# Input projection of a hybrid encoder layer: seven block products in place of eight

## Chip, cores and metric

The kernel runs on one core of a Trainium2 chip. The metric is the device time of one execution in microseconds, a median over runs. TensorE is the matmul engine, VectorE (DVE) and ScalarE (ACT) work element by element, GpSimd (POOL) does little here, and SyncE (SP) issues all DMA transfers, in the order of its queue.

## What is computed

One encoder layer over two groups of 1024 tokens (a prompt and a sample) of width 1024. One matmul projects each token to 8736 columns, which four kinds of heads share; each runs a recurrence in both directions, and a second matmul, a layer norm and a gated input follow.

```
proj = jnp.einsum('btd,de->bte', x, w_in)          # 1024 x 1024 by 1024 x 8736, per group
pr, ph, pm, ps = jnp.split(proj, SPLITS, axis=-1)
mixed = jnp.concatenate([
    _retention(pr, ...),   # 4 heads: q, k (rotated), v, g
    _hgrn2(ph, ...),       # 4 heads: q, zf, zb, i, g
    _mlstm(pm, ...),       # 4 heads: q, k, v, o, g, and 16 gate columns
    _ssd(ps, ...),         # z, x, B, C (a convolution over tokens), and 16 gate columns
], axis=-1)
y = jnp.einsum('bte,ed->btd', mixed, w_out)
x = _layer_norm(DN_ALPHA * x + y, ln_g, ln_b)
gate = sigmoid(x @ w_ple_gate);  return x + gate * (p @ w_ple_proj)
```

## The kernel before

**Precision.** Each fp32 operand of a large matmul is held as two float32r parts, high and low, and a product is three matmuls: high by high, high by low, low by high. `split` (L162) makes the parts: a ScalarE copy for the high one, then a VectorE subtraction for the low one.

**Stages.** For each group the 14 units of `ORDER` (L37) run one after the other: four `hg`, then `ret`, `ssd` and `ml` mixed. A unit projects its own columns, runs its recurrence with fp32 matmuls of 128 columns (two TensorE instructions each, one for a transpose), normalises, transposes and stores 128 channels of the mix to DRAM (`norm_out`, L530; in the rows `hY` is the normalised block, `hZ` the stored one). After both groups come the output projection, layer norm and gate for four half groups.

**Projection.** `stream` (L318) loads a weight piece 512 columns at a time (`ws`) and splits it into `wh` and `wl`; the weights are loaded and split again for the second group. `proj_chan` (L356) gives channels on partitions: the weights are stationary, 512 tokens move, 24 matmuls into one bank `pj`, then an evacuation. `proj_tok` (L341) gives tokens on partitions: the tokens are stationary, 256 weight columns move (288 in `("ret", 0, "vg")`, which carries the gate columns). Retention's pairs, `v` and gates, mLSTM's `v` and `o` and SSD's `z` use the second form. Each bank is one chain of 24 matmuls and is evacuated once.

**Inputs.** `load_x` (L311) loads the 16 blocks of 128 channels by 512 tokens of a group and splits each (`xr` to `xh`, `xl`); the first projection takes them as they come in. `load_mix` does the same for the output stage.

**Order.** A scheduler places all instructions on the engines by priority, which follows the order of the code; `late` (L167) moves a piece, and weight splits go 600 places ahead (`EARLY`). Buffers come from pools: 10 of `p` (1032 columns), 7 of `r`, 12 of `h` (512 columns), 3 pairs of 1024 weight columns, 4 of `ws`, 4 + 4 PSUM banks (L33).

Of the kernel before, what the change touches and what calls it, by code (L numbers as in the profile page):

```python
# [9 lines left out]
F32 = mybir.dt.float32  # L10
# [18 lines left out]
KSC = 128.0 ** -0.5  # L29
ALPHA = 2.0 ** 0.25  # L30
LEVELS = (64, 32, 16, 8)
BLK = 8
PB, RB, HB, WB, SB, SSB = 10, 7, 12, 3, 4, 3  # L33
SLACK = [0, 0]
EARLY = 600
# [4 lines left out]
# column blocks of the input projection  # L40
# [7 lines left out]
def pieces():  # L48
    """(key, columns) of every piece of the input projection, in the order they are used."""
    out = []  # L50
    for g in range(2):
        out.append((("ssd", g, "z"), _blk(O_SSD + 256 * g, 256)))
        out.append((("ssd", g, "x"), _blk(O_SSD + 512 + 256 * g, 256)))
        out.append((("ssd", g, "bc"), _blk(O_SSD + 1024 + 128 * g) + _blk(O_SSD + 1280 + 128 * g)))
    for h in range(4):
        o = O_RET + 128 * h
        out.append((("ret", h, "qk"), _blk(o) + _blk(o + 512)))
        vg = _blk(o + 1024) + _blk(o + 1536)
        if h == 0:
            vg = vg + _blk(O_ML + 2560, 16) + _blk(O_SSD + 1536, 16)  # L60
        out.append((("ret", h, "vg"), vg))
        o = O_HG + 128 * h
        out.append((("hg", h, "qf"), _blk(o) + _blk(o + 512)))
        out.append((("hg", h, "b"), _blk(o + 1024)))
        out.append((("hg", h, "vg"), _blk(o + 1536) + _blk(o + 2048)))
        o = O_ML + 128 * h
        out.append((("ml", h, "qk"), _blk(o) + _blk(o + 512)))
        out.append((("ml", h, "g"), _blk(o + 2048)))
        out.append((("ml", h, "vo"), _blk(o + 1024) + _blk(o + 1536)))
    return out  # L70


IN_PIECES = pieces()
# [3 lines left out]
PIECE_AT = {}  # L77
_off = 0
for _d, _ps in ((D, IN_PIECES), (DI, OUT_PIECES), (D, GATE_PIECES), (PLE, PROJ_PIECES)):
# [8 lines left out]
# columns of the packed shape constants  # L88
K_ID, K_NF, K_NB, K_TF, K_TB, K_RF, K_RB, K_DF, K_DB, K_MF, K_MB = (
    0, 128, 256, 384, 385, 386, 387, 388, 516, 644, 772)  # L90
NKEEP, NCST = 388, 900


def constants():
# [13 lines left out]
    c[:, K_TB] = np.arange(P)  # L108
    m = np.zeros((P, 8, P), np.float32)
# [9 lines left out]
    rope = np.concatenate([cos, sin], 1).reshape(NCH, P, P).transpose(1, 0, 2)  # L119
# [4 lines left out]
def trunk(ctx, tc, xT, x, pT, wp, par_d, cst_d, msk_d, rope_d, out,  # L124
          groups=(0, 1), units=None, tail=True, dbg=None):
# [53 lines left out]
    with ExitStack() as c1:  # L179
        cp = c1.enter_context(tc.tile_pool(name="cp", bufs=1))  # L180
        xp = c1.enter_context(tc.tile_pool(name="xp", bufs=1))
        wq = c1.enter_context(tc.tile_pool(name="wq", bufs=WB))
        st = c1.enter_context(tc.tile_pool(name="st", bufs=SB))
# [30 lines left out]
        cst = par = msk = rope = ident = negm = nhalf = ones = rst = rate = None  # L214
        rrow = rkw = rdec = rD = fbt = ssa = cw = cb = lbw = low = oml = fsc = fbi = ksc = ksum = None

        def setup():
            """Constants, and what depends on the parameters alone."""
            nonlocal cst, par, msk, rope, ident, negm, nhalf, ones, rst, rate, rrow, rkw, rdec, rD
            nonlocal fbt, ssa, cw, cb, lbw, low, oml, fsc, fbi, ksc, ksum  # L220
# [1 line left out]
            cst = cp.tile([P, NKEEP], F32, name="cst")  # L222
            nc.sync.dma_start(cst, cst_d[:, 0:NKEEP])
# [9 lines left out]
            rope = cp.tile([P, NCH, P], F32, name="rope")  # L233
# [1026 lines left out]
```

## Time and profile before

| | us |
|---|---|
| median of 3 runs | 2708.0 (2707.66 to 2711.78) |
| span of the profiled execution | 2708.0 |
| TensorE busy (matmuls) | 2665.3 |
| VectorE busy | 1806.3 |
| ScalarE busy | 1095.3 |
| mean granted TensorE clock | 0.995 |

Busy time is the time in which an engine had an instruction under way; TensorE's matmuls overlap, so what one costs in a row of them is read from the distance between two starts. The granted clock is a share of full speed. The last normalised block of group 0 is written at 1086 us and that of group 1 at 2144 us.

### The profile page before, as it was taken

The numbers are of one execution on the slowest core, as the hardware profiler recorded it, in microseconds if no ns is written. First come the engines' busy times: TensorE is split into PE (matmuls) and PEld (weight loads), VectorE is DVE, ScalarE is ACT, GpSimd is POOL, SyncE is SP. The second block draws the span as 40 slices with busy tenths as digits, with TensorE's granted clock in tenths as the row PEclk, the third lists the DMA queues.
The fourth block names the chain that finished last, engine by engine and source line by source line (L and its number), as shares of the span: only waits on it lengthen the run. The fifth ranks groups of instructions, "written<-read, shape, count | busy, mean of one in ns | idle before, by whom it ended". The sixth has DMA issues, their size and how long they took to land.

```text
span 2708.0 us, 43819 instructions
## 1 busy us (share of the span) xinstructions
PE 2665.3 (98%) x16874; PEld 2384.2 (88%) x16874; DVE 1806.3 (67%) x4417; ACT 1095.3 (40%) x2197; POOL 55.6 (2%) x48
## 2 busy tenths in 40 slices
PE   9999999999999999999999999999999999999999
PEld 8889988879899999999898888989999888888887
DVE  7778768878755555787786878855455555546455
ACT  6656523444422313655533444432222343333323
POOL 0000000000000000000000000000000000000000
PEclk9999999999999999999999999999999999999999
DMA  4111011334321213111111241432122434535333
GB/s 148 47 41 39 24 51 41 94 94 94 86 71 48 78 40 105 44 48 35 41 38 41 75 105 51 91 105 67 56 63 89 164 121 136 190 122 195 128 113 105
DMA packets 172945, 225.15 MB, mean 83 GB/s; under 512 B 13888, under 2 KB 82112, under 8 KB 172736
## 3 DMA queue, kind: packets, MB, share of 16 engines
q1 hardware_dynamic: 172736, 222.34, 27.0%
q8 instruction: 133, 2.18, 0.3%
q14 instruction: 76, 0.62, 0.1%
HBM read 196.86 MB, written 25.43 MB: 82 GB/s over the span
## 4 chain that ended last, share of the span: by engine, by line
PE 93%; DVE 3%; DMA 2%; ACT 1%; issue 1%; POOL 0%; SPq 0%; DVEq 0%; ACTq 0%; POOLq 0%
PE pj L174 53%; PE po L174 13%; PE pg L174 7%; PE pov L177 5%; PE psc L177 5%; PE pst L177 4%; PE ptr L399 3%; PE pin L177 2%; PE pq L174 2%; DMA ub<-ud 1%; DMA ub<-fd 1%; DVE x L160 0%; DMA ws<-in_wp 0%; PE ptl L1125 0%; ACT wh L148 0%
## 5 line engine op out<-in xcount | busy, mean ns | idle before, releaser
L174 PE MATMUL pj<-wl,xh 128*128 128x256 f32 (+1 forms) x2304 | 664.2, 288 | 0.0
L174 PE MATMUL pj<-wh,xh 128*128 128x256 f32 (+1 forms) x2304 | 663.6, 288 | 0.3
L174 PE MATMUL pj<-wh,xl 128*128 128x256 f32 (+1 forms) x2304 | 662.7, 288 | 0.0
L151 DVE TENSOR_TENSOR wl<-ws,wh 128x512 fp32r<-128x512 f32 (+1 forms) x488 | 313.8, 679 | 303.0 <-ACT wh L148 299.8
L148 ACT ACTIVATE wh<-ws 128x512 fp32r<-128x512 f32 (+1 forms) x488 | 280.7, 617 | 468.3 <-PE pj L174 234.4
L174 PEld LDWEIGHTS pj<-wh,xh 128*128 128x128 f32 x2304 | 441.4, 192 | 2.6 <-DVE hB L154 1.1
L174 PEld LDWEIGHTS pj<-wl,xh 128*128 128x128 f32 x2304 | 441.6, 192 | 1.4
L174 PEld LDWEIGHTS pj<-wh,xl 128*128 128x128 f32 x2304 | 441.6, 192 | 0.6
L174 PE MATMUL pj<-xh,wh 128*128 128x512 f32 x1024 | 415.9, 406 | 5.8 <-ACT wh L148 5.8
L174 PE MATMUL pj<-xh,wl 128*128 128x512 f32 x1024 | 414.7, 405 | 0.0
L174 PE MATMUL pj<-xl,wh 128*128 128x512 f32 x1024 | 413.3, 404 | 0.0
L174 PEld LDWEIGHTS pj<-xh,wh 128*128 128x128 f32 x1024 | 194.2, 190 | 40.6 <-ACT wh L148 5.8
L174 PEld LDWEIGHTS pj<-xl,wh 128*128 128x128 f32 x1024 | 194.3, 190 | 34.7
L174 PEld LDWEIGHTS pj<-xh,wl 128*128 128x128 f32 x1024 | 194.1, 190 | 34.7 <-DVE wl L151 0.2
L174 PE MATMUL po<-wl,xh 128*128 128x512 f32 x512 | 202.9, 396 | 0.0
L174 PE MATMUL po<-wh,xh 128*128 128x512 f32 x512 | 202.1, 395 | 0.0
L174 PE MATMUL po<-wh,xl 128*128 128x512 f32 x512 | 202.1, 395 | 0.0
L174 PE MATMUL pg<-xn,wh 128*128 128x512 f32 x384 | 120.2, 394 | 0.0
L174 PEld LDWEIGHTS po<-wl,xh 128*128 128x128 f32 x512 | 96.2, 188 | 21.0
L174 PEld LDWEIGHTS po<-wh,xl 128*128 128x128 f32 x512 | 96.2, 188 | 20.4
L174 PEld LDWEIGHTS po<-wh,xh 128*128 128x128 f32 x512 | 96.2, 188 | 20.0 <-DVE g L157 0.2
L151 DVE TENSOR_TENSOR xl<-xr,xh 128x512 fp32r<-128x512 f32 x96 | 63.9, 690 | 68.5 <-ACT xh L148 66.5
(285 smaller groups left out, 4262.6 us busy)
## 6 DMA issues: line engine op xcount, KB each, us to landing
ws<-in_wp SPq DMA_DIRECT2D x472, 256.0 KB, 3.3
mix<-hZ SPq DMA_DIRECT2D x64, 256.0 KB, 2.8
ub<-fd SPq DMA_DIRECT2D x64, 256.0 KB, 7.3
ub<-ud SPq DMA_DIRECT2D x64, 256.0 KB, 7.1
xr<-mix SPq DMA_DIRECT2D x64, 256.0 KB, 5.1
xr<-in_xT SPq DMA_DIRECT2D x32, 256.0 KB, 5.1
xr<-in_x SPq DMA_DIRECT2D x32, 256.0 KB, 5.0
out<-sg SPq DMA_DIRECT2D x32, 256.0 KB, 2.0
```

Source lines behind the costliest of these rows:

```text
L148: S.activation(o, i, AF.Copy, scale=scale)
L151: V.tensor_tensor(o, a, b, op)
L174: TE.matmul(o, l, r, start=start, stop=stop)
L177: TE.matmul(o, l, r, start=start, stop=stop)
L399: TE.transpose(o[0:s.shape[1], P * n:P * n + s.shape[0]], s, ident[0:s.shape[0], 0:s.shape[0]])
```

## The change

**Seven products.** The input of a group is cut in four blocks (512 channels by 512 tokens: 11 and 12 for the first half of the tokens, 21 and 22 for the second), and the weights of two column blocks of 128 (a "quad") in four as well. Strassen's method, in Winograd's form, needs seven products of such blocks in place of eight: 11, 12, 22 and four sums S1 to S4 of input blocks, each with a weight block or a sum of them. There are 34 quads per group. A product is 12 matmuls of 512 columns with the weights stationary, so all results have channels on partitions.

```diff
+        def quad(g, key, ev_a, ev_b):
+            ws = quad_weights(key, g != groups[0])
+            def product(acc, b, start):
+                w = next(ws)
+                for j in range(4):
+                    h, l = X[b, j]
+                    wh, wl = w[:, P * j:P * j + P], w[:, 512 + P * j:512 + P * j + P]
+                    TE.matmul(acc, wh, h, start=start and j == 0, stop=False, skip_group_check=True)
+                    TE.matmul(acc, wh, l, start=False, stop=False, skip_group_check=True)
+                    TE.matmul(acc, wl, h, start=False, stop=j == 3, skip_group_check=True)
...
+            def held(acc):
+                t = sq.tile([P, 512], F32, tag="sq", name=nm("sq"))
+                with late(-EVAC):
+                    copy(t, acc)
+                return t
...
+            a, b = bank(), bank()
+            product(a, "11", True)
+            u1 = held(a)
+            product(b, "12", True)
+            ev_a(0, put(b, u1, ALU.add))
+            product(a, "S2", False)
+            u2 = held(a)
+            c = bank()
+            product(c, "S1", True)
+            product(a, "S3", False)
+            u3 = held(a)
+            ev_b(1, put(c, u3, ALU.subtract))
+            product(a, "22", False)
+            ev_a(1, put(a))
+            product(c, "S4", False)
+            ev_b(0, put(c, u2, ALU.subtract))
```

Bank `a` goes on adding after each of three copies to SBUF (`sq`, ScalarE); `put` combines two banks' sums in a VectorE addition or subtraction.

**Inputs.** `prep_x` takes the place of `load_x`. It loads 16 blocks, forms S1 to S4, splits seven kinds of blocks by four (tiles `X`) and the block 21, and computes the 32 gate columns by matmuls of their own. It stands ahead of the first unit of a group; the tiles `X` have one buffer each.

```diff
+            for j in range(4):
...
+                put("22", j, r22)
+                t = wq.tile([P, 1024], F32R, tag="w", name=nm("x21"))
+                split(t[:, 0:512], t[:, 512:1024], r21)
+                a = st.tile([P, 512], F32, tag="ws", name=nm("xs"))
+                tt(a, r21, r22, ALU.subtract)
+                put("S1", j, a)
+                tt(a, a, r11[j], ALU.subtract)
+                put("S2", j, a)
+                tt(r12[j], r12[j], a, ALU.add)
+                put("S4", j, r12[j])
+                tt(r11[j], r11[j], r21, ALU.subtract)
+                put("S3", j, r11[j])
```

**Weights.** In group 0 each quad loads four raw blocks, forms three sums in four additions, and splits seven tiles of 512 columns; each split tile (`w`, high and low, 512 KB) is also stored to DRAM (`wd`). In group 1 the seven tiles are loaded from there, with no split.

```diff
+            if cached:
+                for n in range(7):
+                    w = wq.tile([P, 1024], F32R, tag="w", name=nm("w"))
+                    with late(-EARLY):
+                        nc.sync.dma_start(w.bitcast(F32), wd[key][n])
+                    yield w
+                return
...
+            def parts(n, s):
+                w = wq.tile([P, 1024], F32R, tag="w", name=nm("w"))
+                with late(-EARLY):
+                    split(w[:, 0:512], w[:, 512:1024], s)
+                nc.sync.dma_start(wd[key][n], w.bitcast(F32))
+                return w
```

**The units.** What needs tokens on partitions is transposed after the projection (`to_tok`: retention's, HGRN2's and mLSTM's `v`, mLSTM's `o`, SSD's `z`). Retention's rotation runs channel-major, with the halves swapped by four DMAs per half (`sw`). The gates `g` go to DRAM (`gd`, `mg`) and come back in `norm_out`, where the gate is applied channel-major after the transpose. SSD's convolution runs on a padded row of 1028 columns in SBUF in place of two banks. The third quad of each `hg` carries the gate of one mLSTM head.

**Pools and output stage.**

```diff
-PB, RB, HB, WB, SB, SSB = 10, 7, 12, 3, 4, 3
+PB, RB, HB, WB, SB, SSB, QB = 6, 6, 8, 3, 6, 3, 3
-EARLY = 600
+EARLY, EVAC = 600, 400
```

A weight tile `w` now holds 512 columns (high and low side by side), also in the output stage, whose matmuls are the same.

**In the built order.** The names: `pj` a projection bank, `w` and `wh`, `wl` weight parts, `X` and `xh`, `xl` input parts; `ws`, `xr`, `x21`, `x22`, `x12` raw loads; `xs` a sum of inputs. First TensorE, at the end of a projection bank of the first `hg` unit, before:

```order
L174 MATMUL pj_73_448<-xh_57_208,wh_68_412 128x512
L174 MATMUL pj_73_448<-xl_58_209,wh_68_412 128x512
L174 MATMUL pj_73_448<-xh_57_208,wl_69_413 128x512
L174 MATMUL pj_132_704<-wh_124_684,xh_4_98 128x256 [waits Activation_49]
L174 MATMUL pj_132_704<-wl_125_685,xh_4_98 128x256 [waits DVE_49]
L174 MATMUL pj_132_704<-wh_124_684,xl_5_99 128x256
```

and after, in the first quad of the second unit, where the product with S3 ends (`w_286`) and the one with block 22 begins (`w_290`):

```order
L460 MATMUL pj_272_1501<-X_56_277,w_286_1587 128x512
L461 MATMUL pj_272_1501<-X_56_277,w_286_1587 128x512
L462 MATMUL pj_272_1501<-X_56_277,w_286_1587 128x512
L460 MATMUL pj_272_1501<-X_23_152,w_290_1614 128x512 [waits Activation_49]
L461 MATMUL pj_272_1501<-X_23_152,w_290_1614 128x512
L462 MATMUL pj_272_1501<-X_23_152,w_290_1614 128x512 [waits DVE_49]
```

Before, the next chain goes into another bank; after, it goes into the same bank 272, behind a wait for ScalarE.

VectorE at the start of the program, before:

```order
L151 TENSOR_TENSOR xl_5_99<-xr_6_100,xh_4_98 128x512 [waits DMAHW0_49,Activation_49]
L151 TENSOR_TENSOR wl_8_105<-ws_9_106,wh_7_104 128x512 [waits DMAHW1_49,Activation_49]
L151 TENSOR_TENSOR wl_8_105<-ws_10_110,wh_7_104 128x512 [waits DMAHW2_49,Activation_49]
L151 TENSOR_TENSOR xl_12_115<-xr_13_116,xh_11_114 128x512 [waits DMAHW3_49,Activation_49]
L151 TENSOR_TENSOR xl_15_121<-xr_16_122,xh_14_120 128x512 [waits DMAHW4_49,Activation_49]
L151 TENSOR_TENSOR xl_18_127<-xr_19_128,xh_17_126 128x512 [waits DMAHW5_49,Activation_49]
```

and after, the rows up to the first two weight splits (`w_70`, `w_73`):

```order
L157 TENSOR_TENSOR X_50_257<-x22_49_255,X_50_257 128x512 [waits DMAHW3_49,Activation_49]
L157 TENSOR_TENSOR x21_51_260<-x21_48_253,x21_51_260 128x512 [waits DMAHW2_49,PE_49]
L157 TENSOR_TENSOR xs_52_263<-x21_48_253,x22_49_255 128x512
L157 TENSOR_TENSOR X_53_265<-xs_52_263,X_53_265 128x512 [waits Activation_49]
L157 TENSOR_TENSOR xs_52_263<-xs_52_263,x11_17_138 128x512 [waits DVE_49]
L157 TENSOR_TENSOR x12_19_143<-x12_19_143,xs_52_263 128x512 [waits DVE_49]
L157 TENSOR_TENSOR w_70_316<-ws_69_314,w_70_316 128x512 [waits DMAHW4_49,PE_49,Activation_49]
L157 TENSOR_TENSOR X_54_269<-xs_52_263,X_54_269 128x512 [waits Activation_49]
L157 TENSOR_TENSOR w_73_336<-ws_72_334,w_73_336 128x512 [waits DMAHW5_49,PE_49,Activation_49]
```

Before, a weight split (`wl_8`) stands right behind the first input split; after, the first one stands behind 44 operations of 512 columns on the inputs, of which the last six are shown.

SP's queue in group 1, at the end of the first `hg` units, before:

```order
L330 DMA ws_2225_15153<-in_wp 128x512 [waits DMAHW3_49,DVE_49]
L330 DMA ws_2226_15157<-in_wp 128x512 [waits DMAHW4_49,DVE_49]
L330 DMA ws_2229_15163<-in_wp 128x512 [waits DMAHW5_49,DVE_49]
L330 DMA ws_2230_15167<-in_wp 128x512 [waits DMAHW6_49,DVE_49]
L413 DMA mix1_94<-hZ_2094_14300 128x512 [waits Activation_49]
L413 DMA mix1_94<-hZ_2098_14312 128x512 [waits Activation_49]
L330 DMA ws_2249_15345<-in_wp 128x512 [waits DMAHW7_49,DVE_49]
L330 DMA ws_2250_15349<-in_wp 128x512 [waits DMAHW0_49,DVE_49]
```

and after:

```order
L405 DMA w_2216_11904<-wd_hg_2_0_2180 128x1024 [waits DMAHW7_49,PE_49]
L405 DMA w_2218_11920<-wd_hg_2_0_2180 128x1024 [waits DMAHW0_49,PE_49]
L405 DMA w_2219_11935<-wd_hg_2_0_2180 128x1024 [waits DMAHW4_49,PE_49]
L511 DMA gd_2075_11166<-sp_2156_11641 128x512 [waits DVE_49]
L511 DMA mg_2076_11167<-sp_2163_11691 128x512 [waits DVE_49]
L511 DMA gd_2075_11166<-sp_2165_11708 128x512 [waits DMAHW1_49,Activation_49]
L405 DMA w_2222_11952<-wd_hg_2_0_2180 128x1024 [waits DMAHW3_49,DMAHW2_49,PE_49]
L511 DMA mg_2076_11167<-sp_2167_11725 128x512 [waits DVE_49]
L405 DMA w_2223_11966<-wd_hg_2_0_2180 128x1024 [waits DMAHW5_49,PE_49]
L405 DMA w_2225_11984<-wd_hg_2_0_2180 128x1024 [waits DMAHW6_49,PE_49]
```

Before, a weight load waits for VectorE to have split an older one; after, it waits for TensorE to be done with a tile, and `w_2222` stands behind stores of gates that wait for VectorE and ScalarE.

## Rows read from the trace of the kernel before

**Rows 1.** The page: busy time by engine, and the chain that ended last.
```profile
PE 2665.3 (98%) x16874; PEld 2384.2 (88%) x16874; DVE 1806.3 (67%) x4417; ACT 1095.3 (40%) x2197; POOL 55.6 (2%) x48
...
PE 93%; DVE 3%; DMA 2%; ACT 1%; issue 1%; POOL 0%; SPq 0%; DVEq 0%; ACTq 0%; POOLq 0%
```

**Rows 2.** Windows from the trace: busy us (instructions) by engine, clock, DMA share, GB/s.
```profile
0.00:1086.40 1086.40, 1064.13 (x7231) 972.88 (x7232) 765.29 (x1993) 460.35 (x955) 23.41 (x18) 1.00 0.24 69
1086.40:2144.70 1058.30, 1044.14 (x7150) 956.18 (x7149) 744.69 (x1938) 433.28 (x898) 23.16 (x14) 0.99 0.22 64
2144.70:2708.00 563.30, 557.03 (x2496) 455.14 (x2494) 296.28 (x488) 201.66 (x345) 9.08 (x16) 1.00 0.44 146
```

**Rows 3.** Waits, of TensorE: total us, times, longest.
```profile
PE pov L177 <- DVE ub L154: 7.0, 4, 1.8
```

**Rows 4.** Timeline of TensorE: start us, duration us, line, operation (mixed stretches).
```profile
395.49 0.39 PE L174 MATMUL pj<-xh,wh 128*128 128x512 f32 x1
...
401.83 0.39 PE L174 MATMUL pj<-xl,wh 128*128 128x512 f32 x1
...
348.21 0.28 PE L174 MATMUL pj<-wl,xh 128*128 128x256 f32 x1
...
350.85 0.28 PE L174 MATMUL pj<-wh,xl 128*128 128x256 f32 x1
...
712.34 1.03 PE L399 MATMUL ptr<-cst,y 128*128 128x128 f32 x8
```

**Rows 5.** Start of the program: a piece of the chain, and TensorE's first row.
```profile
1.18 3.96 DMA ws<-in_wp
...
5.84 0.79 PE L174 MATMUL pj<-xh,wh 128*128 128x512 f32 x1 [5.84 <-ACT wh L148]
```

**Rows 6.** Groups of VectorE rows: count | busy us, mean ns | idle before.
```profile
L151 DVE TENSOR_TENSOR wl<-ws,wh 128x512 fp32r<-128x512 f32 x472 | 307.0, 686 | 302.8 <-ACT wh L148 299.8 <-PE pj L174 1.6
L154 DVE TENSOR_TENSOR hB<-pj,rope 128x256 f32<-128x256 f32 x64 | 24.1, 412 | 0.0
L154 DVE TENSOR_TENSOR hX<-g,rs 128x512 f32<-128x512 f32 x32 | 22.0, 687 | 24.9 <-POOL rs L406 24.9
L157 DVE TENSOR_SCALAR g<-pj 128x256 f32<-128x256 f32 x56 | 23.3, 419 | 52.8 <-ACT v L148 52.8
L151 DVE TENSOR_TENSOR ub<-ub,ub 128x512 f32<-128x512 f32 x32 | 21.8, 682 | 0.0
L154 DVE TENSOR_TENSOR hA<-pj,rope 128x512 f32<-128x512 f32 x32 | 21.8, 681 | 4.0 <-PE pj L174 4.0
L151 DVE TENSOR_TENSOR k<-hA,hB 128x128 f32<-128x128 f32 x64 | 15.7, 282 | 0.0
L151 DVE TENSOR_TENSOR ob<-ob,pov 128x512 f32<-128x512 f32 x16 | 11.0, 686 | 1.4 <-PE pov L177 1.2
```

**Rows 7.** Groups of ScalarE rows, same columns.
```profile
L148 ACT ACTIVATE q<-pj 128x512 f32<-128x512 f32 x32 | 19.1, 597 | 51.9 <-PE pj L174 51.7
```

**Rows 8.** Windows, the densest 200 us of VectorE.
```profile
400.00:600.00 200.00, 190.71 (x1164) 166.73 (x1163) 162.54 (x486) 85.62 (x207) 4.91 (x3) 0.99 0.28 73
```

**Rows 9.** DMA issues: KB each, median us from issue to landing.
```profile
ws<-in_wp SPq DMA_DIRECT2D x472, 256.0 KB, 3.3
...
ub<-fd SPq DMA_DIRECT2D x64, 256.0 KB, 7.3
...
rope<-in_rope SPq DMA_DIRECT2D x1, 512.0 KB, 5.4
```

**Rows 10.** A wait of TensorE, and windows of TensorE around it.
```profile
353.91 1.11 PE L399 MATMUL ptr<-cst,hY 128*128 128x128 f32 x4 [2.78 <-DVE hY L154]
...
350.00:355.00 5.00, 2.22 (x14) 0.86 0.51 147
355.00:360.00 5.00, 4.28 (x18) 0.50 0.57 198
360.00:365.00 5.00, 5.00 (x39) 0.95 0.00 0
```

More of the change, by code (lines that the diff above doesn't have):

```diff
@@ L124, in trunk @@
 def trunk(ctx, tc, xT, x, pT, wp, par_d, cst_d, msk_d, rope_d, out,
-          groups=(0, 1), units=None, tail=True, dbg=None):
+          groups=(0, 1)):
     nc = tc.nc
@@ new lines, in to_tile, with to_dram, ev, to_tok @@
+        def to_tile(t, func=None, scale=1.0):
+            return lambda hf, put: put(t[:, 512 * hf:512 * hf + 512], func, scale)
+        def to_dram(d):
+            def ev(hf, put):
+                t = ht("sp")
+                put(t)
+                nc.sync.dma_start(d[:, 512 * hf:512 * hf + 512], t)
+            return ev
+        def to_tok(fin):
+            def ev(hf, put):
+                t = ht("vt")
+                put(t)
+                fin(hf, transpose4([t[:, P * n:P * n + P] for n in range(4)]))
+            return ev
@@ L386, in silu @@
-        def silu(x):
-            for hf in range(2):
-                v = x[:, 512 * hf:512 * hf + 512]
+                w = wq.tile([P, 1024], F32R, tag="w", name=nm("w"))
+                s = st.tile([P, 512], F32, tag="ws", name=nm("ws"))
+                nc.sync.dma_start(s, src[:, k * n:k * n + 512])
+                with late(-EARLY):
+                    split(w[:, 0:512], w[:, 512:1024], s)
+                for r in range(kw):
+                    yield w[:, r * n:r * n + n], w[:, 512 + r * n:512 + r * n + n]
@@ L390, in silu @@
+        def silu(x, half=True):
+            for o in range(0, x.shape[1], 512):
+                v = x[:, o:o + 512]
                 e = ht("e")
-                act(e, v, AF.Tanh)
+                act(e, v, AF.Tanh, scale=1.0 if half else 0.5)
                 stt(v, e, 1.0, v, ALU.add, ALU.mult)
@@ L1169, in trunk @@
[L1169 to L1177 removed]
+        for i, g in enumerate(groups):
+            gk = prep_x(g)
+            for j, (b, n) in enumerate(ORDER):
+                if j == 1:
+                    RW.update(gate_rows(g, gk))
+                todo[b](g, n)
@@ L1178, in trunk @@
+        for k in range(2 * NKT):
+            load_mix(groups[0], 0, k)
         blocks = [(g, hf) for g in groups for hf in range(2)]
         def parts(last):
-            if last:
-                h = [xp.tile([P, 512], F32R, tag=f"xh0{k}", name=nm("nh")) for k in range(NKT)]
-                l = [xp.tile([P, 512], F32R, tag=f"xl0{k}", name=nm("nl")) for k in range(NKT)]
-                return h, l
-            both = []
-            for _ in range(2):
-                two = [pt("xn", F32R) for _ in range(4)]
-                both.append([two[k // 2][:, 512 * (k % 2):512 * (k % 2) + 512] for k in range(NKT)])
@@ L1189, in parts @@
-            return both
+            both = [xp.tile([P, 1024], F32R, tag=f"X{k if last else 16 + k}", name=nm("nx")) for k in range(NKT)]
+            return [a[:, 0:512] for a in both], [a[:, 512:1024] for a in both]
         pend = None
```

549 lines of the change are left out of this document (258 added, 291 removed).

## Prediction

> **What bounds the kernel now.** I read the page first. The profiled execution took 2708.0 us, which is also the median of the runs, so a sum made against the one holds for the other. TensorE is busy for 98% of it, VectorE for 67%, ScalarE for 40%, and the chain that ended last is 93% TensorE [rows 1]. Then three windows: group 0 up to its last normalised block (1086.4 us), group 1 up to its last (2144.7 us), and the output stage. In the first two VectorE works 765.3 and 744.7 us of 1086.4 and 1058.3 [rows 2]. Waits confirm it: the longest total for which TensorE stood for another engine is 7.0 us [rows 3]. So each TensorE instruction taken away shortens the kernel, as long as VectorE, the buffers and the transfers keep pace. In group 0 they have 321 us to spare on VectorE; that number decides this case.
>
> **1. TensorE's own work.** The paces are start to start [rows 4]: 512 columns, (401.83 - 395.49) / 28 = 0.2264 us; 256 columns, (350.85 - 348.21) / 22 = 0.120; eight transposes take 1.03 us together, at most 0.129 each, and about 0.11 when the tail of the last (some 0.16, as in the 512-column rows) is taken off. Removed: 3072 of 512 columns, 695.5 us; 6528 of 256, 783.4; 384 of 288 at 0.135 (scaled by columns), 51.8. Together 1530.7. Added: 34 quads x 2 groups x 7 products x 12 matmuls = 5712, and 64 for the gate columns: 5776 x 0.2264 = 1307.7. The results come out channel-major, so 320 transposes of `vt` come in where 64 of retention's `q` go: 256 x 0.11 = 28; a few small ones for the gates, 3.7. Net -191 us, 95.5 per group. (An eighth of 1531 is 191 as well: the transposes and gate columns eat what the dearer 256-column form, 0.120 for half of 0.2264, gives on top.)
>
> **2. The start.** Now the first product can start when one weight tile and one input tile are in: TensorE begins at 5.84 us, after a transfer of 3.96 us [rows 5]. The new order on VectorE has 44 operations of 512 columns ahead of the first weight split (seven input blocks and the sums S1 to S4), and the first product waits for that split: 5 + 44 x 0.65 + about 3 of small setup = 37 us; 0.65 is 307.0 / 472, the pitch of splits in a row [rows 6]. TensorE meanwhile has the gate matmuls, 7 us, counted above. Extra idle 37 - 6 - 7 = 24, taken as 25; between 0, if the sums were hidden, and 30.
>
> **3. The wait for a held copy.** A quad adds products into one bank `a`, and a copy has to leave the bank before the next product goes in. After the first and second there is another bank's product (12 x 0.2264 = 2.7 us) between; after S3 comes block 22 into the same bank. A ScalarE evacuation of 512 columns takes 0.597 us [rows 7]; the matmul's drain is 0.39 - 0.23 = 0.16 [rows 4], and I allow 0.14 for two signals: 0.9 us. In the new TensorE order 25 of 68 quads have nothing between S3 and 22, and 20 more have less than 0.9 us; the shortfalls add up to 30 us, 13 in group 0 and 17 in group 1. Bounds: 0, if those copies are early, and 46 at 1.2 us each.
>
> **4. VectorE in group 0.** From 765.3 us: 132 weight splits of 512 and 8 of 288 columns go, -89. In come 34 x 7 splits at 0.65, +155; four block sums of weights per quad, 136 at 0.68 (the SBUF-only row), +92; three combinations per quad out of PSUM, 102 at 0.686, +70; 32 more operations on the inputs, +21 [rows 6]. Retention's rotation loses half of its rows' busy time, 38.5 (`hA`, `hB`, `k`, and `q` like `k`), and gets 48 x 0.68 = 33; the gates' evacuation and scaling by `rs` lose about 25 and gain 12 for the product at the store; the rest (convolution in whole rows, `kw` and `v` moved to ScalarE) loses some 26: -45. Sum 969 us. TensorE alone would need 1086.4 - 95.5 + 25 + 13 = 1029. So VectorE would have to work 94% of the time, with queues in fixed order and with fewer buffers (`p` 10 to 6, `h` 12 to 8). No long stretch shows that: the densest 200 us has 162.5, 81%, though there TensorE set the pace [rows 8]. Bounds for group 0: 1029, and 969 / 0.81 = 1196. I take 1050 (92%), nearer the first, since that 81% was not VectorE's own limit. Here most waits of step 3 disappear inside VectorE's.
>
> **5. Between the groups.** The 48 operations on the inputs wait for the last quad's products, and with retention's last 20 us on VectorE they are 32 + 20; TensorE has 17 us of leftover and gates. Some splits of blocks 11 and 12 start earlier, so 20 us; between 0 and 35. In group 1 VectorE has no splits: 744.7 - 89 + 70 + 21 - 45 = 702 of about 1030, no bound.
>
> **6. Group 1's weights from DRAM.** 238 tiles of 512 KB replace 136 of 256 KB and less, with three buffers: a load can start when product n - 3 is done and must land before n. By the new order that window has a median of 6.4 us (two products, 5.4, and what stands between). A 256 KB load lands in 3.3 us, the one 512 KB load in 5.4, the slow broadcasts in 7.3 [rows 9]. Adding up the shortfalls over all windows: 1 us at 3.3, 14 at 5.4, 100 at 6.5, 204 at 7.3. SP issues in order, and a load now stands behind stores that wait for other engines. I take somewhat above 5.4: 35 us, and keep 1 and 204. The Trainium skill (DMA: Bandwidth & Descriptors, Anatomy of one DMA) gives 2.0 us plus bytes / 436e3, which would be an estimated 3.2 us; by that the term would be about 1 and the sum 34 less. The one such load in this trace took 5.4, so the row speaks for the higher value.
>
> **7. The output stage** keeps its matmuls. Its weight tiles are half as wide with as many buffers, and the split is prefetched less far: +5, between 0 and 20.
>
> **Sum.** Group 0 1050; group 1 1058.3 - 95.5 + 20 + 17 + 35 = 1035; output 563.3 + 5 = 568. Together 2653; I say 2650, 2% less. Two thirds of the saving in TensorE's work would be given back.
>
> **Rivals.** (a) All covers hold: group 0 at 1030, group 1 at 1000 (loads at 5.4 us, copies early): 2598. For it: ScalarE has room, and the orders put splits early. Against it: step 4 at 94%.
> (b) **Slower by VectorE.** Group 0 runs at the densest density seen, 81%: 1196 and 2799 in all. It turns slower than now when group 0 goes over 1050 + 55 = 1105, that is when VectorE works under 88%. For it: fewer buffers, and each split is a ScalarE copy and then a VectorE subtraction. Against it: nothing in the trace shows VectorE bound below 100%.
> (c) **Slower by loads.** Each 512 KB load takes 7.3 us with what it waits for on SP: 35 becomes 204, 2822. It turns slower at a term of 90, some 6.4 us a load. For it: two loads overlap, at 512 KB in 2.7 us. Against it: the transfer engines are 22% busy in group 1 now [rows 2].
> (d) **The clock.** After TensorE had waited 2.78 us for VectorE at 351, the granted clock was 0.50: the shares of 0.86, 0.50 and 0.95 in three stretches of 5 us make 6.9 us at half speed [rows 10], a cost of 3.5 us a time. A group 0 with 10 to 15 such waits adds about 45: 2698. The Trainium skill (TensorE: Matmul & The Clock Gate, What's actually happening) says that the clock is throttled by default and that activity releases it, which agrees with the 0.50 behind that wait; by that rule a VectorE-bound stretch costs TensorE twice.
>
> **How the numbers follow.** Forecast 0.40 (its own range 2610 to 2695), (a) 0.20, (b) 0.17, (c) 0.13, (d) 0.10. Faster by over 0.2% (about what a measurement of this kernel can tell) takes the forecast, (a), and over half of (d): 0.66. Within 0.2%: 0.05. Slower: (b), (c) and the rest of (d): 0.29. The range goes from 2575 (a little under (a)) to 2780, which leaves out the far ends of (b) and (c).
>
> **What would show it.** `pj` matmuls 5712, all of 512 columns, at 0.226 us; VectorE near 970 us in group 0 and 700 in group 1; the first product near 37 us; TensorE's waits led by held copies (`sq`), by splits in group 0 and by DMA of `w` in group 1. I am wrong if VectorE stays under 85% in group 0 with no loss, if loads of `w` land well above 6 us, or if the paces change.

## The result and the profile after

The changed kernel takes 3073.2 us (median of 4 runs, 3065.4 to 3079.3) where the kernel before takes 2708.7: a ratio of 1.134, with a 95% interval of 1.132 to 1.136. It is 13.4% slower; I had forecast 2% faster.

The page of the changed kernel, its first lines (to be laid beside [rows 1]):

```profile
span 3071.3 us, 37562 instructions
PE 2681.8 (87%) x12954; PEld 2186.9 (71%) x12954; DVE 1981.7 (65%) x4374; ACT 1209.4 (39%) x2294; POOL 60.5 (2%) x80
...
PEclk8898999969779898899899997979989899999999
...
PE 68%; DVE 13%; DMA 10%; ACT 4%; issue 3%; SPq 1%; POOL 1%; DVEq 0%; ACTq 0%; POOLq 0%
```

TensorE executes 12954 matmuls and not 16874, and yet is busy longer, 2681.8 us against 2665.3. It also stands for 3071.3 - 2681.8 = 389.5 us, where it stood for 42.7. The line of the clock shows the main reason why it is busy longer: it has sevens and one six. The chain that ended last is 68% TensorE, no longer 93%.

The windows of the three stages (length, busy time and count of each engine, granted clock, DMA share, GB/s), as [rows 2]:

```profile
0.00:1301.50 1301.50, 1077.20 (x5188) 868.91 (x5188) 967.06 (x2162) 568.52 (x1113) 26.55 (x34) 0.88 0.51 167
1301.50:2502.70 1201.20, 1043.75 (x5244) 856.70 (x5245) 712.01 (x1720) 429.37 (x833) 25.30 (x30) 0.92 0.50 151
2502.70:3071.30 568.60, 560.88 (x2524) 461.28 (x2522) 302.62 (x494) 211.53 (x349) 8.68 (x16) 1.00 0.45 144
```

Group 0 takes 1301 us (forecast 1050), group 1 takes 1201 (1035), the output stage 568.6 (568). VectorE's work is what I had summed up, 967 and 712 us, but neither group runs at its pace: it is busy for 74% and 59%. In both groups the granted clock is well under 1.

TensorE's waits (who waits for what: us in total, times, longest), where [rows 3] had 7.0 us at the top:

```profile
PE ptr L549 <- DVE k L157: 79.7, 13, 11.3
PE pin L183 <- DVE S L166: 62.4, 43, 4.2
PE psc L183 <- DVE a L160: 43.8, 31, 2.2
PE pov L183 <- DVE ub L160: 23.4, 16, 3.8
PE pj L460 <- ACT sq L154: 19.9, 30, 1.4
PE pj L460 <- DVE sp L157: 15.9, 8, 2.0
PE pj L460 <- DVE vt L157: 13.4, 4, 3.8
...
PE pj L460 <- DMA w<-wd_ssd: 3.5, 1, 3.5
...
PE pj L460 <- DMA w<-wd_ml: 2.5, 1, 2.5
...
PE pj L460 <- DMA w<-wd_ret: 2.1, 1, 2.1
...
PE pj L460 <- DMA w<-wd_hg: 1.2, 2, 0.6
```

The first four are inside the units' own chains: retention's rotated `k`, SSD's states `S`, HGRN2's levels `a`, the broadcast rows `ub`; together 209 us. The projection itself (`pj`) waits less, 68 us: 19.9 for held copies, 29.3 until VectorE has combined two banks (`sp`, `vt`), 9.3 for loaded weights, and the rest for weight splits.

One SSD state chain shows the mechanism. Stretches of TensorE's timeline (start, length, instruction, count, idle time before it and what ended it), first of the kernel before, then of the changed one:

```profile
501.19 0.59 PE L177 MATMUL pin<-S,C 128*128 128x256 f32 x2
501.62 0.59 PE L177 MATMUL pst<-xw,xs 128*128 128x256 f32 x2
501.86 0.58 PE L174 MATMUL pj<-xh,wl 128*128 128x512 f32 x1
...
504.12 0.40 PE L174 MATMUL pj<-xh,wl 128*128 128x512 f32 x1
504.35 0.60 PE L177 MATMUL pin<-S,C 128*128 128x256 f32 x2
```

```profile
625.90 1.19 PE L183 MATMUL pin<-S,C 128*128 128x256 f32 x2 [1.04 <-DVE S L166]
626.88 1.06 PE L183 MATMUL pst<-xw,xs 128*128 128x256 f32 x2
628.99 1.19 PE L183 MATMUL pin<-S,C 128*128 128x256 f32 x2 [1.04 <-DVE S L166]
629.97 1.06 PE L183 MATMUL pst<-xw,xs 128*128 128x256 f32 x2
632.07 1.19 PE L183 MATMUL pin<-S,C 128*128 128x256 f32 x2 [1.04 <-DVE S L166]
```

A step of the chain takes 504.35 - 501.19 = 3.2 us before and 628.99 - 625.90 = 3.1 us after: the chain was always there. Before, ten projection matmuls stood between `pst` and the next `pin`, so TensorE was never seen waiting. Now nothing stands there, and each matmul takes twice as long. In TensorE's order the four chains, from first to last `pin`, hold 150, 181, 150 and 181 projection matmuls before, and 6, 0, 26 and 24 after. Windows from the first to the last `pin` of the first chain, of before and of after, and of after's second:

```profile
467.20:508.00 40.80, 38.83 (x205) 33.25 (x205) 33.33 (x135) 14.52 (x41) 0.00 (x0) 1.00 0.42 110
```

```profile
615.50:657.60 42.10, 25.25 (x60) 15.13 (x60) 33.39 (x136) 9.95 (x30) 0.00 (x0) 0.59 0.31 89
816.50:861.00 44.50, 27.27 (x54) 15.82 (x55) 31.36 (x129) 9.37 (x30) 0.00 (x0) 0.50 0.25 55
```

The length is about the same; 205 matmuls lay in it before, 60 now, and the granted clock went from 1.00 to 0.59 and 0.50.

**The account.** At full clock TensorE should have been busy for 2665.3 - 191 = 2474 us. It was busy for 2681.8: 207 us more. It stood for 347 us more than before. So 207 + 347 - 191 = +363, the difference of the two spans (3071.3 - 2708.0). Most of the 207 is half clock, but not all: in the trace TensorE is busy for 342 us at a granted clock of 0.50, where it was for 22 before, and half of the difference is 160 us. The other 47 are not clock. An estimated 37 of them are the ends of bursts: the last matmul of a row runs on for some 0.16 us (0.39 - 0.23 [rows 4]), which counts as busy, and the trace has 265 idle gaps where it had 34.

### The profile page after: what moved, and what is told of

Read it like the earlier page. It is cut to its first block, busy times and chain, and to the rows that moved or that the text cites. A ratio compares the mean times of both kernels' runs of the same rounds, so it can differ in the third digit from the quotient of the medians.

```text
span 3071.3 us, 37562 instructions
## 1 busy us (share of the span) xinstructions
PE 2681.8 (87%) x12954; PEld 2186.9 (71%) x12954; DVE 1981.7 (65%) x4374; ACT 1209.4 (39%) x2294; POOL 60.5 (2%) x80
## 4 chain that ended last, share of the span: by engine, by line
PE 68%; DVE 13%; DMA 10%; ACT 4%; issue 3%; SPq 1%; POOL 1%; DVEq 0%; ACTq 0%; POOLq 0%
PE po L180 11%; PE pj L460 11%; PE pj L462 11%; PE pj L461 10%; PE pg L180 6%; PE pov L183 5%; PE psc L183 5%; DMA ub<-ud 3%; PE ptr L549 3%; PE pst L183 2%; PE pin L183 2%; DMA ub<-fd 2%; PE pq L180 1%; DMA sw<-q 1%; DVE w L157 1%
## 5 line engine op out<-in xcount | busy, mean ns | idle before, releaser
L460 PE MATMUL pj<-X,w 128*128 128x512 f32 x1904 | 786.3, 413 | 67.8 <-ACT sq L154 19.9
L461 PE MATMUL pj<-X,w 128*128 128x512 f32 x1904 | 772.0, 405 | 0.0
L462 PE MATMUL pj<-X,w 128*128 128x512 f32 x1904 | 767.4, 405 | 0.4 <-DVE w L157 0.4
L154 ACT ACTIVATE w<-ws 128x512 fp32r<-128x512 f32 x412 | 259.4, 630 | 570.8 <-PE pj L462 201.6
L460 PEld LDWEIGHTS pj<-X,w 128*128 128x128 f32 x1904 | 367.4, 193 | 158.4 <-ACT sq L154 35.9
L157 DVE TENSOR_TENSOR w<-ws,w 128x512 fp32r<-128x512 f32 x412 | 283.6, 689 | 291.5 <-ACT w L154 286.6
L462 PEld LDWEIGHTS pj<-X,w 128*128 128x128 f32 x1904 | 366.4, 192 | 69.7 <-DVE w L157 0.8
L461 PEld LDWEIGHTS pj<-X,w 128*128 128x128 f32 x1904 | 366.9, 193 | 64.4
L180 PE MATMUL po<-w,X 128*128 128x512 f32 x1536 | 364.8, 396 | 0.1
L180 PEld LDWEIGHTS po<-w,X 128*128 128x128 f32 x1536 | 285.9, 188 | 62.6 <-issue 1.2
L154 ACT ACTIVATE sq<-pj 128x512 f32<-128x512 f32 x204 | 120.2, 589 | 243.0 <-PE pj L462 234.5
L180 PE MATMUL pg<-nx,w 128*128 128x512 f32 x768 | 178.2, 391 | 1.0 <-ACT lm L151 1.0
L183 PE MATMUL psc<-a,k 128*128 128x128 f32 x768 | 129.7, 321 | 51.9 <-DVE a L160 43.8
L180 PEld LDWEIGHTS pg<-nx,w 128*128 128x128 f32 x768 | 145.1, 189 | 31.5 <-ACT lm L151 1.3
L183 PE MATMUL pin<-S,C 128*128 128x256 f32 x112 | 57.9, 614 | 63.3 <-DVE S L166 62.4
L549 PE MATMUL ptr<-cst,k 128*128 128x128 f32 x128 | 22.4, 313 | 80.7 <-DVE k L157 79.7
```

What stands on the lines that cost most here:

```text
L154: S.activation(o, i, AF.Copy, scale=scale)
L157: V.tensor_tensor(o, a, b, op)
L180: TE.matmul(o, l, r, start=start, stop=stop)
L183: TE.matmul(o, l, r, start=start, stop=stop)
L460: TE.matmul(acc, wh, h, start=start and j == 0, stop=False, skip_group_check=True)
L461: TE.matmul(acc, wh, l, start=False, stop=False, skip_group_check=True)
```

## The experiments

**Theory (lost cover).** The units' chains wait for VectorE, ScalarE and DMA, SSD's as long as it did before; the projection used to fill these waits, and the changed order no longer does. TensorE stands, and its clock falls. One chain is longer than it was: retention's rotation now passes through DMA (x2). **Rivals:** (buffers) too few tiles; (b) VectorE's load; (c) loads; (d) the clock by itself; and (units) the channel-major rewrite, apart from the method. All edits are to the changed kernel unless said otherwise.

**x1_pools.** Buffers as before.

```diff
-PB, RB, HB, WB, SB, SSB, QB = 6, 6, 8, 3, 6, 3, 3
+PB, RB, HB, WB, SB, SSB, QB = 10, 7, 12, 3, 6, 3, 3
-                put("S4", j, r12[j])
+                X["S4", j] = X["12", j]     # S3 likewise
```

> The changed kernel with the buffers of the kernel before (p 10, r 7, h 12). To make room, the blocks S3 and S4 are not made: products S3 and S4 read block 12, and 8 input splits per group are left out; all matmuls, weight splits and sums stay. Theory 'buffers': TensorE's 390 us of idle time and the half clock behind it come from tiles that are not free; they mostly go, group 0 falls from 1301 to near 1100 and group 1 from 1201 to near 1020, 2690 to 2750 in all. Rival 'order': the program's order on TensorE hardly changes (6, 0, 26 and 24 products inside the four SSD state chains, as now), so the chains stay bare: less than 100 us faster, 2975 to 3070.

3012.9 us, 60 less, and 8 input splits a group are gone too. So for the most part TensorE doesn't wait for free tiles. That the order counts in their place is argued here and tested in x14 and x15.

**x2_swap.** The half swap of the rotation.

```diff
-                    nc.sync.dma_start(y[0:64, :], x[64:P, sl])
-                    nc.sync.dma_start(y[64:P, :], x[0:64, sl])
+                    copy(y[0:64, :], x[64:P, sl])
+                    copy(y[64:P, :], x[0:64, sl])
```

> The changed kernel with retention's half swap (sw) made by two ScalarE copies from the other 64 partitions in place of two DMAs. Theory 'rotation': the 13 waits of ptr for k (79.7 us) shrink to under 20, and with the clock behind them the kernel is 70 to 110 us faster, 2965 to 3005. Rival 'VectorE is late anyway': the waits stay on k, because the products with cos and sin stand late in VectorE's queue: under 30 us, 3045 or more.

2996.9 us, 76 less, with 36.8 of the 79.7 us of waits left; I had expected under 20. The wait for `k` and the copies:

```profile
PE ptr L549 <- DVE k L157: 36.8, 10, 6.4
```

```profile
L154 ACT ACTIVATE sw<-k x32: 627/630/632, 515.3 to 2384.3; 64x512 f32<-64x512 f32 x32
```

The gain (76) is larger than the 43 us of waits for `k` that went: other waits shrink as well (idle time falls by 56 us, to 333.4), and busy time falls by 16, some 14 of it clock.

**x3_load.** No weight splits but the first quad's.

```diff
+            if wd.get("one"):
+                key = wd["one"]
-            ws = quad_weights(key, g != groups[0])
+            ws = quad_weights(key, "one" in wd)
+            wd["one"] = key
```

> The changed kernel in which only the first quad splits and stores its weights; every other quad of both groups loads that quad's seven tiles of 512 KB from DRAM. Left out: 33 quads' weight splits, block sums and stores. VectorE then has about 255 us less to do in group 0. Rival 'VectorE bound' (b): group 0 falls from 1301 to near 1050, 2820 in all. Theory 'lost cover': group 0 falls no lower than group 1 already stands with the same work, 1180 to 1240, so 2950 to 3010 in all. Rival 'loads' (c): the same loads now hurt group 0 as well, no gain, 3060 to 3100.

2965.7 us, 107 less. Its group 0:

```profile
0.00:1218.50 1218.50, 1047.74 (x5217) 853.15 (x5217) 752.18 (x1813) 455.97 (x896) 25.86 (x34) 0.91 0.47 152
```

VectorE has 215 us less to do there (967 to 752), and group 0 falls by 83, to about where group 1 stood (1201). So VectorE's load has a price, 107 us of the 365 in all, but it is not what bounds group 0: without these 215 us of it, 1218 us remain. The loads that were added are not free; they show as a new wait:

```profile
PE pj L463 <- DMA w<-wd_hg: 18.1, 12, 3.0
```

**x4_classic.** Eight products in the same units.

```diff
-            a, b = bank(), bank()
-            product(a, "11", True)
-            u1 = held(a)
...
+            for ev in (ev_a, ev_b):
+                a, b = bank(), bank()
+                w = next(ws)
+                product(a, "11", w, True)
+                product(b, "21", w, True)
+                w = next(ws)
+                product(a, "12", w, False)
+                ev(0, put(a))
+                product(b, "22", w, False)
+                ev(1, put(b))
```

> The changed kernel with eight block products in place of seven: each quad's four banks take two products each, in pairs that share a weight tile; no block sums, no held copies, no combinations out of two banks; four stored tiles a quad, not seven. Buffers, channel-major units, gates through DRAM and the rotation by DMA stay. TensorE gets 68 x 12 x 0.2264 = 185 us more. Rival 'channel-major units' (the rewrite, not the method): the waits stay, 3200 to 3260. Theory 'the method takes the cover away' (every second product needs VectorE and a tile to free its bank): the SSD chains hold 51 to 54 products where they held 0 to 26, the idle time falls by half or more and the clock recovers: 2850 to 2980, faster than the changed kernel in spite of more matmuls.

2939.1 us: 134 less with 185 us more of matmuls. Its page and longest waits:

```profile
PE 2748.7 (94%) x13770; PEld 2276.3 (78%) x13770; DVE 1672.5 (57%) x3868; ACT 1116.7 (38%) x2138; POOL 57.7 (2%) x80
```

```profile
PE pin L183 <- DVE S L166: 54.2, 26, 4.8
PE ptr L518 <- DVE k L157: 50.7, 11, 7.9
```

Idle time falls from 389.5 to 2936.8 - 2748.7 = 188.1 us. But the kernel before does about the same matmul work in 2708: the rewritten units and the fewer buffers, without the method, cost 231.

**x5_z.** SSD's `z` quad ahead of the state loop.

```diff
+            z = [pt("z")[:, 0:T] for _ in range(2)]
+            with late(0):
+                ev = [...]
+                quad(g, ("ssd", s2, 2), *ev)
             S = [None, None]
             for n in range(NCH - 1):
...
-            z = [pt("z")[:, 0:T] for _ in range(2)]
-            ev = [...]
-            quad(g, ("ssd", s2, 2), *ev)
```

> The changed kernel with one thing moved: SSD's third quad (z) stands in the program ahead of the loop of states, not behind the scores. On TensorE the four state chains then hold 144, 135, 117 and 117 product matmuls where they held 6, 0, 26 and 24. Nothing is added or left out. Theory 'lost cover': some 115 us of products (513 - 56 = 457 x 0.2264 = 103 us) go into time in which TensorE stood or ran at half clock; the 62 us of waits of pin for S fall under 20: 70 to 120 us faster, 2950 to 3000. Rival: the products were cover where they stood before (scores, norm), and the waits only move: under 30 us, 3040 or more.

3016.1 us, 57 less: between the two. The first chain is covered (45.2 us busy of 45.2, clock 1.00), but the quad had been cover where it stood:

```profile
620.30:665.50 45.20, 45.20 (x199) 36.82 (x199) 40.51 (x147) 17.70 (x42) 0.00 (x0) 1.00 0.73 216
```

```profile
PE ptr L549 <- DVE y L160: 39.9, 4, 10.7
...
PE pin L183 <- DVE S L166: 11.3, 4, 4.1
```

`pin`'s waits fall from 62.4 to 11.3, and a new wait of 39.9 us opens at SSD's norm (`y`). Idle time is 383.2, hardly less; busy time falls by 51, and nearly all of that is clock (48). Cover was moved, not made.

**x6_moves.** The swap, `z`, and two more quads moved ahead of the work that their unit does next.

```diff
+            quad(g, ("hg", h, 2), to_dram(gd), to_dram(RW["mg", h]))
             prs = []          # HGRN2's levels begin
...
+            quad(g, ("ret", h, 1), to_tok(...), to_dram(gd))
             kws = [v3(rt("kw")[:, 0:T]) for d in range(2)]   # rotation begins
```

> The move of x5_z, the swap of x2_swap, and two more moves in the changed kernel: HGRN2's third quad ahead of the levels, retention's second quad ahead of the rotation. 'Lost cover': the gains of the swap (76 us) and of z (70 to 120) add up, and the two moves take some more of the waits of psc for a (44 us) and ptr for k (37 us left): 2800 to 2920. If what is left is VectorE's order or the held copies, the moves add nothing to the first two: 2880 to 2930.

2915.4 us, 158 less, the best time with the whole of the method; the two moves add 25 to the 76 and 57. The time lies in both of the ranges that I had given, so this run does not tell the two apart.

**x7_classic_zs.** x4 with the edits of x2 and x5.

```diff
+                    copy(y[0:64, :], x[64:P, sl])     # x2_swap, in x4_classic
+            quad(g, ("ssd", s2, 2), *ev)              # ahead of the states, x5_z
```

> Eight products as in x4_classic (2939 us), with SSD's z quad ahead of the state loop and the swap on ScalarE. The SSD chains hold 123, 123, 110 and 110 products where x4_classic has 51 to 54. 'Lost cover': with eight products and the same units most of the 181 us of idle time goes, and TensorE's work is that of the kernel before less 6 us: 2760 to 2840. Rival 'channel-major units': 2880 or more.

2834.8 us, 104 less than x4. With the same units and buffers, and with two moves more, seven products (x6) are 81 us slower than eight.

**x8_idle_products.** Matmuls that compute nothing, in the state chains.

```diff
                 po = ps("pin")
+                for _ in range(3):
+                    TE.matmul(po, X["11", 0][0][:, 0:P], X["11", 0][0], start=True, stop=True)
                 mm(po[:, 0:256], CT[:, P * c:P * c + P], S, True, True)
```

> The changed kernel with three matmuls of 512 columns ahead of each SSD matmul pin, into the same bank, whose result pin overwrites: 336 matmuls that compute nothing, 76 us of work, put into the waits of the state chains. Rival (d) 'the clock itself': the chains' 195 us at half clock come back as 95 us, 2980 or less. Theory 'lost cover': the chains run at VectorE's pace, so the clock gives back only what stands behind the chain (scores, pov at half rate), 10 to 50 us, 3020 to 3060. If the added matmuls stand in the way: 3075 or more.

3045.7 us, 28 less, with 38 us more of matmuls: the trace has 168 more (13122 against 12954), half of the 336 that I had counted. Its first chain, and the wait behind it:

```profile
607.00:638.30 31.30, 25.58 (x112) 19.71 (x112) 27.56 (x127) 2.93 (x7) 0.00 (x0) 1.00 0.38 98
```

```profile
PE pov L183 <- DVE ub L160: 47.3, 21, 5.8
```

At clock 1.00 the chain takes 31.3 us and not 42.1, and the four together 124 and not 168. I had expected VectorE's pace to hold them at their length; that part was wrong: VectorE is busy for 33.4 of the 42.1 us, since in each step it waits for matmuls at half rate. The waits for `ub` right behind the chains then grow by 24 us and take back over half of the 44. So the clock costs time by itself (d), but here its recovery, less what the added matmuls cost, is 28 us of 365.

**x9_no_sum_out, x10_no_held, x11_products_only.** The method's own operations, taken out one kind after the other.

```diff
-                        if t is not None:
-                            tt(dst, acc, t, op)
-                        elif func is None:
+                        if func is None:              # x9: a ScalarE copy only
...
-                with late(-EVAC):
-                    copy(t, acc)
-                return t
+                return None                           # x10: x9 and no held copy
                                                       # x11: x10 with the edit of x3_load
```

> The changed kernel in which every bank of a quad leaves TensorE's memory by one ScalarE copy: the 204 VectorE combinations of a bank with a held copy are left out (204 x 0.686 = 140 us of VectorE), ScalarE gets as many copies; the held copies are still made, though nothing reads them. It divides what the method costs against x4_classic (3073 and 2939 - 185 = 2754 for equal TensorE work: 319 us). Theory 'VectorE's latency': a bank is late because its combination stands in VectorE's queue behind chains: 80 to 160 us faster, 2910 to 2995. Rival 'weight tiles' (12 matmuls a tile, where x4 has 24): under 40 us, 3035 or more.

> x9_no_sum_out without the 204 held copies too: the products of bank a follow each other with no copy between. Left out: combinations and held copies. My step 3 gave the held copies 30 us of waiting; the trace has 19.9 us of pj for sq. With the clock behind it I expect 20 to 60 us less than x9, 2860 to 2960. If the copies were hidden: as x9 within 10 us.

> x10_no_held and x3_load in one: seven products from loaded tiles, and nothing else of the method (left out: combinations, held copies, the splits, sums and stores of all quads but the first). Theory 'VectorE's latency': what the method adds on VectorE and ScalarE is the 319 us, so this comes to 2754 and, as x4 still has four splits a quad in group 0, somewhat less: 2700 to 2790. Rival 'weight tiles': seven tiles of 12 matmuls each, with three buffers, still cost over 100 us: 2860 or more.

3004.8, 2968.5 and 2892.7 us: the combinations cost 68 (less than I expected), the held copies 36, the splits, sums and stores 76. x11 is the surprise: my range (2700 to 2790) missed it, and the rival's holds it. It has 185 us less of matmuls than x4, no weight splits but the first quad's, and gains 46:

```profile
PE 2604.7 (90%) x12954; PEld 2145.7 (74%) x12954; DVE 1628.6 (56%) x3807; ACT 1072.8 (37%) x2047; POOL 56.2 (2%) x80
```

```profile
PE ptr L545 <- DVE k L157: 55.2, 12, 7.2
PE pin L183 <- DVE S L166: 52.4, 33, 4.0
PE pov L183 <- DVE ub L160: 30.6, 16, 4.3
PE pj L463 <- DMA w<-wd_hg: 29.9, 14, 4.5
PE psc L183 <- DVE a L160: 20.7, 20, 1.7
```

Its idle time is 2890.1 - 2604.7 = 285.4 us, 97 more than x4's. Matmuls were taken away, and waits took their place, but not all of them in the units' chains: of the 97, `psc` and `pov` have 35 (the wait of `psc` for `a` is 1.9 us in x4), the projection 33, of which 29.9 are loads of `w` (none in x4), the gate matmuls at the inputs 22, the start of the output stage 12 (a few others shrink). So lost cover is shown for a part of them, and loads are another.

**x12_weight_tiles.**

```diff
-PB, RB, HB, WB, SB, SSB, QB = 10, 7, 12, 3, 6, 3, 3     # x1_pools
+PB, RB, HB, WB, SB, SSB, QB = 10, 7, 12, 7, 7, 3, 3
```

> x1_pools (3013 us) with seven weight tiles in place of three, and seven raw ones in place of six; for the room the block S2 isn't made either, so products S2, S3 and S4 read other blocks. Rival 'weight tiles': TensorE's waits are quads whose weights come late: 2950 or less. Theory 'VectorE's latency': the waits name VectorE's results, not w (9 us of ACT, 9 us of DMA): within 25 us of x1, 2990 to 3035.

3005.0 us, 8 less than x1, and the splits of S2 are gone too: in the changed kernel the number of weight tiles isn't it. For x11, which loads in both groups, this run does not rule the rival out.

**x13_classic_zs_pools.** x7 with the pools of the kernel before.

```diff
-PB, RB, HB, WB, SB, SSB, QB = 6, 6, 8, 3, 6, 3, 3
+PB, RB, HB, WB, SB, SSB, QB = 10, 7, 12, 3, 6, 3, 3
```

> x7_classic_zs (2835 us) with the tile buffers of the kernel before: p 10, r 7, h 12 in place of 6, 6 and 8 (the four S blocks aren't needed with eight products). Theory 'buffers': the 127 us that are left to the kernel before go for the most part, 2720 to 2770. Theory 'channel-major units' (start at 20.7 us, results combined and turned through more steps, SSD's norm waits for z): 2800 to 2840.

2806.4 us: buffers explain 28 of the 127 us between x7 and the kernel before. The longest wait left is SSD's norm again:

```profile
PE ptr L518 <- DVE y L160: 25.7, 4, 9.6
```

**x14_before_few_buffers, x15_before_four_p.** The kernel before, with tiles held back until the last block of group 1 is stored.

```diff
+        hold += [pt("hold") for _ in range(4)] + [rt("hold") for _ in range(1)] + [ht("hold") for _ in range(4)]
...                                    # x15: range(6) for pt, range(0) for rt and ht
```

> The kernel before with four p, one r and four h tiles held back until the last block of group 1 is stored, so that p 6, r 6 and h 8 are left in the groups, as in the changed kernel; nothing else but nine small sums at the end. The order on TensorE stays as it was but for a few instructions (the four SSD chains hold 150, 176, 150 and 176 products). Theory 'buffers': waits for free tiles cost 100 us or more, 2810 up. Theory 'order': 2705 to 2760.

> The kernel before with six p tiles held back, four left in the groups. HGRN2 needs five a block, so no block's projection can be done under the levels of the block ahead: on TensorE the levels of one block (56 groups of four matmuls) have 95 products among them, where the four blocks together had 1191 among 224. No work is added but six small sums. Theory 'lost cover': with the very work of the kernel before the levels run bare, with waits of psc for a, and the clock falls behind them: 2800 to 3000. Rival: the method's extra work is what costs, and cover is cheap: under 2760.

2723.0 us (ratio 1.006, 1.005 to 1.008) and 2820.7 (1.041, 1.040 to 1.043). With the changed kernel's buffers and its own order the kernel before loses 15 us. With an order that takes cover from the levels (95 product matmuls between the first and the last `psc` for `a` of a block, in its trace, where 138 to 178 stood) it loses 112, doing the same work. The page and first waits of x15:

```profile
PE 2709.8 (96%) x16874; PEld 2420.8 (86%) x16874; DVE 1811.6 (64%) x4429; ACT 1096.6 (39%) x2197; POOL 55.2 (2%) x48
```

```profile
PE psc L177 <- DVE a L154: 46.9, 24, 3.1
PE psc L177 <- ACT k L145: 19.3, 16, 2.1
```

TensorE stands for 68 us more, nearly all of it in these two waits, and is busy for 45 more, some 38 of them half clock, out of a chain that showed no wait in [rows 3]. Of all runs this one shows most directly what lost cover costs.

**The ladder.** Each line differs from the one above by the step named; "above the sum" is busy time over 2665 us (the kernel before), 2659 (eight products) or 2474 (seven), and "half clock" is the part of it that the trace's granted clock explains.

| kernel | us | step | idle | above the sum | half clock |
|---|---|---|---|---|---|
| before | 2708 | | 43 | 0 | 0 |
| x13 | 2806 | channel-major units: +98 | 111 | 34 | 11 |
| x7 | 2835 | fewer buffers: +28 | 133 | 44 | 25 |
| x4 | 2939 | `z` behind the chains, swap by DMA: +104 | 188 | 90 | 74 |
| x11 | 2893 | seven products, and no splits: -46 | 285 | 130 | 101 |
| x10 | 2968 | splits, sums, stores: +76 | 322 | 168 | 134 |
| x9 | 3005 | held copies: +36 | 350 | 188 | 137 |
| after | 3073 | combinations: +68 | 390 | 207 | 160 |

Idle time grows at every step, the one that saves 185 us of matmuls too. The steps are prices in this order, not independent ones: the swap and `z` gave 76 and 57 on the changed kernel, together 104 on x4. The first step has all that came with the units: inputs prepared ahead, gates through DRAM, group 1's weights from DRAM. The step to x11 also has its added loads.

## Why the prediction was wrong

**The step that failed stands ahead of the sum**: "So each TensorE instruction taken away shortens the kernel, as long as VectorE, the buffers and the transfers keep pace." I read [rows 3] as "TensorE waits for nobody"; they say only that the waits were covered. What covered them were the matmuls that the change removes and moves, and I took no term for it. In its place the runs showed that work taken from TensorE comes back as standing and half clock: 185 us fewer matmuls were worth 46 us (x4 against x11, loads included), and the kernel before lost 112 us by its order alone (x15). I priced the resources of VectorE (a sum of busy time) and never its latency inside a chain. The numbers were within reach: the same order that gave me the 45 close copies shows 6, 0, 26 and 24 products in the state chains, where 150 to 181 stood. A second term that I put at nothing is the way of the rotated halves through DMA: step 4 has the rotation's work on VectorE and no wait, and x2 shows 76 us for it.

**1. TensorE's own work: right, and worth little.** The first of the three rows of products, each 1904 times (5712 together); at full clock one lasts 389 ns, as before:

```profile
L460 PE MATMUL pj<-X,w x1904: 387/389/796, 39.8 to 2470.4; 128*128 128x512 f32 x191
```

The 191 us did leave TensorE. x4 against x11 shows what the 185 of them that the method saves bring: 46, even with the splits gone, though part of the rest went to the loads that x11 adds.

**2. The start: right.** The first product starts at 39.8 us; I had 37.

**3. Held copies: right in kind.** 30 waits, 19.9 us in all, where I had 45 and 30 us. Without the copies the kernel gains 36 us (x10 against x9), clock included.

**4. VectorE in group 0: the sum right, the conclusion wrong.** 967 us against 969 predicted; but group 0 took 1301, outside both my bounds (1029 and 1196), with VectorE at 74%. x3 takes 215 us of it away, and 83 come back.

**5. Group 1, "no bound": wrong**, and the clearest sign. VectorE has 712 us (702 predicted) in 1201 us. No throughput explains that. x15 shows such a loss with nothing of the change in it: its group 1 takes 1109.7 us, with the work that took 1058.3.

**6. Loads: mis-sized to the safe side.**

```profile
w<-wd_hg SPq DMA_DIRECT2D x84, 512.0 KB, 3.4
...
w<-wd_ret SPq DMA_DIRECT2D x56, 512.0 KB, 3.8
```

A load lands in 3.4 to 3.8 us (medians), and TensorE waits 9.3 us for them, near my lower bound of 1 and not 35. I had taken the one row of 5.4 us, which was a single load [rows 9]. The Trainium skill (DMA: Bandwidth & Descriptors, Anatomy of one DMA) gives its fit, an estimated 3.2 us here, for DMAs that GpSimd issues, which I did not say; these loads are issued by SyncE, and still the fit was nearer than the 5.4.

**7. Output stage: right**, 568.6 against 568.

**The rivals.** (b) and (c) named the right side and the wrong cause. (d) had the right mechanism, at 45 us; it measured about 160, since I counted 10 to 15 waits with 3.5 us each and did not see that a bare chain stays at half clock for much of its length. My range (2575 to 2780) left out any case in which the chains themselves came to light.

**What stays open.** 98 us of the units (x13 against the kernel before, with equal `p`, `r` and `h` tiles and about equal matmul work) are named by the trace only: a later start (the first product at 20.7 us, not 5.8, some 7 us of which are the gate matmuls that now stand ahead of it), 25.7 of SSD's norm, 12.2 of `pov` for `ub` (7.0 before [rows 3]) and smaller waits, and 34 of busy time above the sum, of which 11 are half clock. No run took them apart. Nor did a run tell how the method's share (x4 against the changed kernel) falls to lost cover and to VectorE's added work, which the ladder takes out together with the waits that it causes. No version faster than the kernel before came out of this: the best with the whole method is x6, 2915.

## What to carry to other kernels

When a page shows one engine busy for 98% and no waits, the waits may only be covered: before taking work from that engine, list the chains that pass through it, and count in the old and the new order how much independent work stands inside each. A saving counts where the engine has nothing that waits; from inside a covered chain, work taken away came back here as idle time, and as clock too. A change in the method should leave the order of the units as it was, or be measured first with the old method in the new order, as x4 did here.

## What the runs showed of the hardware

The granted clock went down to 0.50 (1.2 of 2.4 GHz) and stayed there with waits that are mostly short: in the second state chain a `pin` and a `pst` come together, with waits of 1.0 to 1.1 us between most of these pairs and 3.8 at the longest, and the clock is 0.50 for all of the 44.5 us. The other three, with 6, 26 and 24 product matmuls among them, had 0.59, 0.71 and 0.68. In x8, with three more matmuls ahead of each `pin`, all four chains ran at 1.00. Matmuls of no use kept the engine at full speed, and the kernel came out 28 us faster. The Trainium skill (TensorE: Matmul & The Clock Gate, What's actually happening) says that activity releases the throttle, and this pair of runs agrees; nothing in my reading of [rows 10], one wait of 2.78 us, told that a row of such waits keeps it low. Two ScalarE copies of 64 x 512 between halves of the partitions, 0.63 us each, took the place of transfers that landed in over 4 us:

```profile
sw<-q SPq DMA_DIRECT2D x32, 128.0 KB, 4.4
sw<-k SPq DMA_DIRECT2D x32, 128.0 KB, 4.1
```
